# Hybrid decoder layer, one core: longer modelled waits and held order of the small products in the mixing stage

## The chip, the cores and the metric

One core of one Trainium2 chip runs the whole layer. The metric is device time in microseconds of one execution, the median of several runs; lower is better. Beside it stands one profiled execution, whose span and instructions the rows below show.

## The reference

The layer computes, in float32, for 512 tokens of 1024 columns: a SwiGLU half step, a mixing sub-layer of two branches, a second half step and a final norm. The mixing sub-layer is what the change touches.

```python
x = x + 0.5 * swiglu(rms_norm(x, ffn1_norm), ffn1_w_gate, ffn1_w_up, ffn1_w_down)
h = rms_norm(x, mix_norm)
p_rwkv, p_att, p_gate = split(h @ w_in)
y_rwkv = rwkv7_branch(p_rwkv, ...)     # 8 heads of 64; S_t = S diag(w) + (S a) b^T + v k^T, y = S r
y_att = attention_branch(p_att, ...)   # 8 query heads, 2 key heads, window 128, sinks
merged = sigmoid(gate_rwkv) * (y_rwkv @ w_branch_rwkv) + sigmoid(gate_att) * (y_att @ w_branch_attn)
x = x + merged @ w_out
x = x + 0.5 * swiglu(rms_norm(x, ffn2_norm), ffn2_w_gate, ffn2_w_up, ffn2_w_down)
return rms_norm(x, final_norm)
```

## The kernel before

**Layout.** Activations lie transposed: 128 columns of the layer on the partitions, 512 tokens along the free axis. A float32 product with weights ("dense") is done as three products of rounded parts: each weight tile is split into `wh` (a cast on ScalarE, ACT, L183) and `wl` (a subtraction on VectorE, DVE, L184), and `mm3` (L198 to L205) adds three TensorE (PE) products into one PSUM bank, `mm`. Raw weights come by DMA from the SP queue into three buffers `wr`.

**Stages.** The first half step fills the time to about 366 us, the mixing stage to about 725, the rest of mixing (branch and output projections) to about 816, then the second half step.

**Mixing stage.** The rwkv recurrence runs in blocks of 64 tokens (`C`), with two heads on the two halves of the partitions (h = 0 on 0 to 63, h = 1 on 64 to 127); four pairs of heads in all. Its small products use half or a quarter of the array each. Five generators ("lanes") hold the work:

- `lane_a`: attention's keys (`att_kv`), then four query pairs (`att`, L1178 on): the scores (L1191, L1193) into two banks `pS`, one per half; masking, exponentials, the scaling L1217, transposes (L1225), the output product (L1236, L1240) from `Pc` and `Pp`.
- `lane_p(0)`, `lane_p(1)`: for two pairs of heads each, `prep` (L809) and `solve` (L925). In `prep` the matrix G (L871 to L881) is made in two batches of eight products (four per half, L877), each half into a bank of its own; DVE masks both banks into `GT` (L880). `BK`, the stationary operand, is written for h = 0 and then h = 1 (L857, L862). Transposes of BK (L886) and the centred values `pvv` (L894) follow. `solve` inverts triangular blocks on DVE, with transfers through memory.
- `lane_w(0)`, `lane_w(1)`: `wkv` (L987): products p1 and p2 (L1003, L1012), three groups (L1029 to L1061), `pz` (L1070), six hops one after another (L1081, each followed by an ACT copy, L1083), the output product `py` (L1088, L1092), then the head norm.
- `head_sums` (L784) is used by all: ACT casts `hi` (L787), DVE makes `lo` (L789), and after a modelled wait of `WSUM` = 1200 PE runs L792 and L793.

**PSUM.** The small products share the tag `sm`: three banks for "a" (prep and lane_w(0)), three for "b" (attention and lane_w(1)). Dense products have one bank each of `mma` and `mmb`.

**Dense stream.** `dense_stream` (L707) walks through 42 jobs: k, r, v per pair of heads, K, V, q, sixteen gate tiles g, and eight b (which need attention's output). A job's two or four quarter steps are six products each, and count 1390 on the model's clock. At most two jobs ahead have their weights loaded.

**What sets the order.** `Counted` (L70) issues the small products and adds modelled nanoseconds to a clock. `interleave` (L87 to L108) is the planner: each lane yields a modelled wait and is ready again when the clock has passed it; a ready lane (in the order a, w0, w1, p0, p1) goes on; when none is ready, one dense step is emitted; a step more is emitted for each 3840 of credit. That is the traced order. The Tile scheduler then orders each engine's instructions: an instruction traced earlier goes first unless, in the scheduler's own forecast, its inputs or its buffer aren't ready yet; then a later one takes its place. The engines run that fixed order on the chip and wait wherever an input is late. `tc.keep_in_program_order(i)` binds an instruction behind the one traced just before it on the same engine; others may still come between the two.

The lines of the planner that the change touches:

```python
        wait = next(lanes[i], None)
        ...
        credit += RATIO * (pe.clock - before)
        ready[i] = pe.clock + wait
```

Of the kernel before, what the change touches and what calls it, by code (L numbers as in the profile page):

```python
# [15 lines left out]
P = 128  # L16
# [15 lines left out]
HD = 64  # L32
C = 64
# [22 lines left out]
HOP = 900.0  # L56

# [12 lines left out]
class Counted:  # L70


    def __init__(self, pe):
        self.pe, self.clock = pe, 0.0

    def matmul(self, out, lhsT, rhs, **k):
        self.pe.matmul(out, lhsT=lhsT, rhs=rhs, **k)  # L77

        half = lhsT.shape[0] <= HD or _free(lhsT) <= HD
        self.clock += 4 * max(_free(lhsT) / 2, _free(rhs)) / 2.4 * (0.55 if half else 1.0)  # L80

    def transpose(self, out, in_, ident):
        self.pe.transpose(out, in_, ident)  # L83
        self.clock += 2 * _free(in_) / 2.4


def interleave(lanes, pe, dense):  # L87
# [5 lines left out]
    while live:  # L93
# [11 lines left out]
        ready[i] = pe.clock + wait  # L105
# [13 lines left out]
def hybrid_layer_kernel(  # L119
# [625 lines left out]
    sp = Counted(pe)  # L745
# [63 lines left out]
    def prep(i):  # L809
# [177 lines left out]
    def wkv(i, sx):  # L987
# [12 lines left out]
        for n in range(NCH):  # L1000
            for h in (0, 1):
                r0 = h * HD
                sp.matmul(p1[r0 + 32:r0 + HD, n * 32:(n + 1) * 32], lhsT=GT[r0:r0 + 32, n // 2, h, n % 2, 32:],  # L1003
                          rhs=YTv[r0:r0 + 32, n, :], start=True, stop=True)
# [4 lines left out]
        for n in range(NCH):  # L1009
            for h in (0, 1):  # L1010
                r0 = h * HD
                sp.matmul(p2[r0:r0 + 32, n * 32:(n + 1) * 32], lhsT=YTv[r0 + 32:r0 + HD, n, :],  # L1012
                          rhs=GI[r0 + 32:r0 + HD, n, 32:64], start=True, stop=True)
# [12 lines left out]
        for n in range(NCH):  # L1026
            if n > 0:
                for h in (0, 1):
                    sp.matmul(pa[HS[h], n, :], lhsT=AR[HS[h], n, 0, :], rhs=ident[HS[h], HS[h]], start=True, stop=True)  # L1029
            for h in (0, 1):  # L1030
                sp.matmul(pv_[HS[h], n, :], lhsT=GT[OS[h], n // 2, h, n % 2, :], rhs=UV[OS[h], n, h, :],
                          start=True, stop=True)
# [6 lines left out]
        for n in range(NCH):  # L1039
            for h in (0, 1):  # L1040
                sp.matmul(pv_[HS[h], n, :], lhsT=GI[HS[h], n, :], rhs=xv[HS[h], n, :], start=True, stop=True)
        for n in range(1, NCH):
            for h in (0, 1):
                sp.matmul(pa[HS[h], n, :], lhsT=GI[HS[h], n, :], rhs=at_[HS[h], n, :], start=True, stop=True)
# [10 lines left out]
        for n in range(1, NCH):  # L1055
            for h in (0, 1):
                sp.matmul(pr_[HS[h], n, :], lhsT=AR[HS[h], n, 0, :], rhs=GT[HS[h], n // 2, h, 2 + n % 2, :],
                          start=True, stop=True)
            for h in (0, 1):
                if n + 1 < NCH:  # L1060
                    sp.matmul(pm[HS[h], n, :], lhsT=AR[HS[h], n, 0, :], rhs=GT[HS[h], n // 2, n % 2, 4 + h, :],  # L1061
                              start=True, stop=True)
# [360 lines left out]
```

## Time and profile before

| what | value |
|---|---|
| median of 3 runs | 1161.02 us (1157.81 to 1163.99) |
| profiled execution | 1161.56 us |
| its span in the profile | 1159.8 us |
| PE busy | 1118.2 us |
| DVE busy | 870.4 us |
| ACT busy | 585.7 us |

"Busy" is the time in which at least one instruction of the engine ran. In the names of groups, `sm<-AR,BK` is an output tile, the moving operand and the stationary one; a float32 product appears as two records, a transpose as one. L77 is the line in `Counted.matmul` through which all small products pass, so they are told apart by their tiles; L83 is that of the transposes. "64*128" is the part of the array that a product uses (rows by columns).

### The profile page before, as it was taken

Reading aid. Unit: us, or ns where it says so; the run is one execution under the profiler, and the core shown is the slowest. Engines: PE = TensorE matmul, PEld = TensorE weight load, DVE = VectorE, ACT = ScalarE, POOL = GpSimd, SP = SyncE. Lnnn points to the kernel's source line nnn. Section 1 sums busy time; section 2 is a strip of 40 time slices with the busy share of each in tenths; the row PEclk is TensorE's granted clock in tenths of the full one; section 3 lists DMA queues with packets and bytes.
Section 4 is the critical chain, followed back from the end, with each engine's and each line's share of the span. In section 5 each row is a group of like instructions: output and inputs, shape, how many; then the busy total and the mean of one; then the engine's idle time right before and its main releaser. Section 6 shows DMA issues by size and latency. Waiting matters only on the chain.

```text
span 1159.8 us, 19736 instructions
## 1 busy us (share of the span) xinstructions
PE 1118.2 (96%) x7866; PEld 970.1 (84%) x7866; DVE 870.4 (75%) x1138; ACT 585.7 (50%) x945; POOL 245.1 (21%) x175
## 2 busy tenths in 40 slices
PE   7899999999999999999998999999999999999997
PEld 6698899979987787777776788777999899989985
DVE  6988579856986589988886533878997379945875
ACT  5754155523645755566744445656655145523554
POOL 6231034202301000000111122121432024302200
PEclk9999999999999999999989999999999999999999
DMA  9234233432135534434235425852334223432221
GB/s 272 58 108 128 73 92 109 138 98 73 49 100 166 184 111 97 102 83 122 70 89 148 121 84 156 261 162 83 92 110 143 76 82 101 134 103 73 74 91 73
DMA packets 223068, 130.12 MB, mean 112 GB/s; under 512 B 37727, under 2 KB 204448, under 8 KB 222976
## 3 DMA queue, kind: packets, MB, share of 16 engines
q1 hardware_dynamic: 221248, 126.79, 38.2%
q10 hardware_dynamic: 1184, 2.04, 0.5%
q8 instruction: 62, 1.02, 0.4%
q14 instruction: 30, 0.25, 0.1%
q0 software_dynamic: 544, 0.04, 0.0%
HBM read 112.96 MB, written 15.61 MB: 111 GB/s over the span
## 4 chain that ended last, share of the span: by engine, by line
PE 72%; DVE 17%; DMA 5%; ACT 3%; issue 2%; SPq 1%; POOL 0%; ACTq 0%; DVEq 0%; POOLq 0%
PE sm L418 30%; PE mm L203 9%; PE mm L205 9%; PE mm L204 9%; PE sm L77 4%; PE sm L203 3%; PE sm L205 3%; PE sm L204 3%; DVE wl L184 3%; DVE pr L921 2%; DVE xt L377 1%; ACT wh L183 1%; PE sm L83 1%; DMA wr<-in_ffn_w_up_dram 1%; DMA wr<-in_ffn_w_gate_dram 1%
## 5 line engine op out<-in xcount | busy, mean ns | idle before, releaser
L184 DVE TENSOR_TENSOR wl<-wr,wh 128x1024 fp32r<-128x1024 f32 (+2 forms) x149 | 213.7, 1434 | 93.0 <-ACT wh L183 92.4
L183 ACT CAST wh<-wr 128x1024 fp32r<-128x1024 f32 (+2 forms) x149 | 147.5, 990 | 216.7 <-PE mm L204 98.7
L406 POOL TENSOR_TENSOR wx<-wr,wx 128x1024 f32<-128x1024 f32 x40 | 117.6, 2940 | 371.5 <-DVE wl L184 242.2
L418 PE MATMUL sm<-th,wh 128*128 128x256 f32 x640 | 180.9, 283 | 0.6 <-ACT s L429 0.3
L418 PE MATMUL sm<-tl,wh 128*128 128x256 f32 x640 | 180.2, 282 | 0.0
L418 PE MATMUL sm<-th,wl 128*128 128x256 f32 x640 | 180.2, 282 | 0.0
L184 DVE TENSOR_TENSOR wl<-wx,wh 128x1024 fp32r<-128x1024 f32 x100 | 157.6, 1583 | 26.9 <-ACT wh L183 26.2
L183 ACT CAST wh<-wx 128x1024 fp32r<-128x1024 f32 x100 | 104.9, 1049 | 131.9 <-PE sm L418 80.4
L418 PE MATMUL sm<-xh,wl 128*128 128x256 f32 x480 | 136.0, 283 | 0.8 <-DVE wl L184 0.8
L418 PE MATMUL sm<-xh,wh 128*128 128x256 f32 x480 | 136.0, 283 | 0.0
L418 PE MATMUL sm<-xl,wh 128*128 128x256 f32 x480 | 135.7, 283 | 0.0
L203 PE MATMUL mm<-xh,wh 128*128 128x512 f32 x320 | 130.9, 409 | 3.2 <-ACT wh L183 1.7
L205 PE MATMUL mm<-xh,wl 128*128 128x512 f32 x320 | 126.3, 395 | 1.0 <-DVE wl L184 1.0
L204 PE MATMUL mm<-xl,wh 128*128 128x512 f32 x320 | 126.4, 395 | 0.0
L418 PEld LDWEIGHTS sm<-th,wh 128*128 128x128 f32 x640 | 120.7, 189 | 1.7 <-issue 0.7
L418 PEld LDWEIGHTS sm<-tl,wh 128*128 128x128 f32 x640 | 120.6, 188 | 0.0
L418 PEld LDWEIGHTS sm<-th,wl 128*128 128x128 f32 x640 | 120.5, 188 | 0.0
L418 PEld LDWEIGHTS sm<-xh,wl 128*128 128x128 f32 x480 | 91.8, 191 | 1.3 <-DVE wl L184 1.3
L418 PEld LDWEIGHTS sm<-xh,wh 128*128 128x128 f32 x480 | 91.7, 191 | 0.5 <-issue 0.2
L418 PEld LDWEIGHTS sm<-xl,wh 128*128 128x128 f32 x480 | 91.7, 191 | 0.5 <-issue 0.2
L203 PEld LDWEIGHTS mm<-xh,wh 128*128 128x128 f32 x320 | 60.3, 189 | 19.0 <-issue 2.0
L205 PEld LDWEIGHTS mm<-xh,wl 128*128 128x128 f32 x320 | 60.5, 189 | 15.5 <-DVE wl L184 1.4
(387 smaller groups left out, 2289.8 us busy)
## 6 DMA issues: line engine op xcount, KB each, us to landing
wr<-in_ffn_w_down_dram SPq DMA_DIRECT2D x38, 512.0 KB, 4.0
wr<-in_w_in_dram SPq DMA_DIRECT2D x34, 512.0 KB, 4.2
wr<-in_ffn_w_gate_dram SPq DMA_DIRECT2D x42, 256.0 KB, 3.0
wr<-in_ffn_w_up_dram SPq DMA_DIRECT2D x42, 256.0 KB, 3.4
wx<-in_ffn_w_gate_dram SPq DMA_DIRECT2D x40, 256.0 KB, 3.1
wx<-in_ffn_w_up_dram SPq DMA_DIRECT2D x40, 256.0 KB, 3.5
gd<-gt SPq DMA_DIRECT2D x16, 256.0 KB, 2.3
wr<-in_w_out_dram SPq DMA_DIRECT2D x8, 512.0 KB, 5.5
```

What stands on the lines that cost most here:

```text
L77: self.pe.matmul(out, lhsT=lhsT, rhs=rhs, **k)
L83: self.pe.transpose(out, in_, ident)
L183: s.copy(out=hi[:, c], in_=raw[:, c])
L184: v.tensor_tensor(out=lo[:, c], in0=raw[:, c], in1=hi[:, c].bitcast(F32), op=ALU.subtract)
L203: pe.matmul(acc, lhsT=ah, rhs=bh, start=(first and k == 0), stop=False)
L204: pe.matmul(acc, lhsT=ah, rhs=bl, start=False, stop=False)
L205: pe.matmul(acc, lhsT=al, rhs=bh, start=False, stop=(last and k == n - 1))
L377: v.scalar_tensor_tensor(out=t_[:, 1 + i, :], in0=b0, scalar=g1, in1=b1, op0=ALU.mult, op1=ALU.add if i == 2 else ALU.subtract)
L406: e.tensor_tensor(out=o, in0=a, in1=b, op=op)
L418: pe.matmul(acc, lhsT=x_, rhs=y_, start=first and j == 0 and k == 0 and i == 0, stop=last and k == n - 1 and i == 2, skip_group_check=True)
L921: v.tensor_tensor(out=pv_[:, m], in0=a_[:, m].unsqueeze(2).broadcast_to(sh), in1=b_[:, m].rearrange("p u c -> p c u").unsqueeze(1).broadca ...
```

## The change

A constant `SLACK = 1.15, 200.0` is added, and the planner takes a modelled wait above 300 as 1.15 times the wait plus 200. `Counted` gets the tile context and a context manager `together`: within it, each small product but the first is bound behind the one traced before it. Eleven groups of small products are put into such a block: G's two batches, `pvv`, p1, p2, the four groups of `wkv` up to `pz`, `py`, the scores and the output product of attention. In G and in the first part of attention's output product the halves are traced h = 1 first, then h = 0. No operation is added or removed. The remaining hunks only indent other groups in the same way.

```diff
--- before.py
+++ after.py
@@ -54,6 +54,7 @@
 AHEAD = 2
 WSUM = 1200.0
 HOP = 900.0
+SLACK = 1.15, 200.0
 
 
 class InOrder:
@@ -70,17 +71,30 @@
 class Counted:
 
 
-    def __init__(self, pe):
-        self.pe, self.clock = pe, 0.0
+    def __init__(self, pe, tc):
+        self.pe, self.tc, self.clock, self.lump = pe, tc, 0.0, None
+
+    @contextmanager
+    def together(self):
+
+        self.lump = 0
+        yield
+        self.lump = None
+
+    def keep(self, i):
+        if self.lump is not None:
+            if self.lump:
+                self.tc.keep_in_program_order(i)
+            self.lump += 1
 
     def matmul(self, out, lhsT, rhs, **k):
-        self.pe.matmul(out, lhsT=lhsT, rhs=rhs, **k)
+        self.keep(self.pe.matmul(out, lhsT=lhsT, rhs=rhs, **k))
 
         half = lhsT.shape[0] <= HD or _free(lhsT) <= HD
         self.clock += 4 * max(_free(lhsT) / 2, _free(rhs)) / 2.4 * (0.55 if half else 1.0)
 
     def transpose(self, out, in_, ident):
-        self.pe.transpose(out, in_, ident)
+        self.keep(self.pe.transpose(out, in_, ident))
         self.clock += 2 * _free(in_) / 2.4
 
 
@@ -102,7 +116,7 @@
             live.remove(i)
             continue
         credit += RATIO * (pe.clock - before)
-        ready[i] = pe.clock + wait
+        ready[i] = pe.clock + (SLACK[0] * wait + SLACK[1] if wait > 300.0 else wait)
         while credit >= LUMP:
             d = next(dense, 0.0)
             credit = credit - d if d else 0.0
@@ -742,7 +756,7 @@
             yas.append((h_, l_))
 
     jobs = list(JOBS)
-    sp = Counted(pe)
+    sp = Counted(pe, tc)
     dense = dense_stream()
 
     def need(*whats):
@@ -871,11 +885,12 @@
         GT = slot("GT", (P, NCH // 2, 2, 6, C))
         for n2 in range(0, NCH // 2, 2):
             pg = [pssm().rearrange("p (n a c) -> p n a c", n=2, c=C) for h in (0, 1)]
-            for n in (n2, n2 + 1):
-                for m in (0, 1):
-                    for h in (0, 1):
-                        sp.matmul(pg[h][:, n - n2, m:4:2, :], lhsT=BK[HS[h], 2 * n + m, :, :],
-                                  rhs=AR[HS[h], 2 * n + m, :, :], start=True, stop=True)
+            with sp.together():
+                for n in (n2, n2 + 1):
+                    for m in (0, 1):
+                        for h in (1, 0):
+                            sp.matmul(pg[h][:, n - n2, m:4:2, :], lhsT=BK[HS[h], 2 * n + m, :, :],
+                                      rhs=AR[HS[h], 2 * n + m, :, :], start=True, stop=True)
             for h in (0, 1):
                 v.tensor_tensor(out=GT[:, n2:n2 + 2, h, 0:4, :], in0=pg[h],
                                 in1=gmask.unsqueeze(1).broadcast_to([P, 2, 4, C]), op=ALU.mult)
@@ -889,10 +904,11 @@
         yield 0.0
 
         pvv = pssm()
-        for n in range(NCH):
-            ns = slice(n * C, (n + 1) * C)
-            sp.matmul(pvv[HD:P, ns], lhsT=vm[0:HD, ns], rhs=cen[0:HD, :], start=True, stop=True)
-            sp.matmul(pvv[0:HD, ns], lhsT=vm[HD:P, ns], rhs=cen[HD:P, :], start=True, stop=True)
+        with sp.together():
+            for n in range(NCH):
+                ns = slice(n * C, (n + 1) * C)
+                sp.matmul(pvv[HD:P, ns], lhsT=vm[0:HD, ns], rhs=cen[0:HD, :], start=True, stop=True)
+                sp.matmul(pvv[0:HD, ns], lhsT=vm[HD:P, ns], rhs=cen[HD:P, :], start=True, stop=True)
         UV = slot("UV", (P, NCH, 2, C))
         s.copy(out=UV[HD:P, :, 0, :], in_=c3(pvv)[HD:P])
         v.tensor_copy(out=UV[0:HD, :, 1, :], in_=c3(pvv)[0:HD])
...
@@ -1183,14 +1206,15 @@
         S = slot("S2", (P, 2, NB, P))
         for b2 in (0, 1):
             pS = [pssm("b").rearrange("p (b a c) -> p b a c", b=2, a=2) for h in (0, 1)]
-            for bb in (0, 1):
-                b = 2 * b2 + bb
-                for h in (0, 1):
-                    qs, k_ = qn[HS[h], b * P:(b + 1) * P], kd[(kv + h) % 2][HS[h]]
-                    if b == 0:
-                        sp.matmul(pS[h][:, 0, 1, :], lhsT=qs, rhs=k_[:, 0:P], start=True, stop=True)
-                    else:
-                        sp.matmul(pS[h][:, bb, :, :], lhsT=qs, rhs=k_[:, (b - 1) * P:(b + 1) * P], start=True, stop=True)
+            with sp.together():
+                for bb in (0, 1):
+                    b = 2 * b2 + bb
+                    for h in (0, 1):
+                        qs, k_ = qn[HS[h], b * P:(b + 1) * P], kd[(kv + h) % 2][HS[h]]
+                        if b == 0:
+                            sp.matmul(pS[h][:, 0, 1, :], lhsT=qs, rhs=k_[:, 0:P], start=True, stop=True)
+                        else:
+                            sp.matmul(pS[h][:, bb, :, :], lhsT=qs, rhs=k_[:, (b - 1) * P:(b + 1) * P], start=True, stop=True)
             for h in (0, 1):
                 s.copy(out=S[:, h, 2 * b2:2 * b2 + 2, :], in_=pS[h][:, :, 1, :])
                 for bb in (0, 1):
@@ -1228,17 +1252,18 @@
             s.copy(out=Pp[:, h, 0:3 * P], in_=pT[:, P:4 * P])
         yield 2500.0
         po = pssm("b")
-        for b in range(NB):
-            bs = slice(b * P, (b + 1) * P)
-
-
-            for h in (0, 1):
-                sp.matmul(po[HS[h], bs], lhsT=vdv[:, b, kv * HD:(kv + 1) * HD], rhs=Pc[:, h, bs],
-                          start=True, stop=(b == 0))
-            for h in (0, 1):
-                if b > 0:
-                    sp.matmul(po[HS[h], bs], lhsT=vtv[:, b - 1, kv * HD:(kv + 1) * HD], rhs=Pp[:, h, (b - 1) * P:b * P],
-                              start=False, stop=True)
+        with sp.together():
+            for b in range(NB):
+                bs = slice(b * P, (b + 1) * P)
+
+
+                for h in (1, 0):
+                    sp.matmul(po[HS[h], bs], lhsT=vdv[:, b, kv * HD:(kv + 1) * HD], rhs=Pc[:, h, bs],
+                              start=True, stop=(b == 0))
+                for h in (0, 1):
+                    if b > 0:
+                        sp.matmul(po[HS[h], bs], lhsT=vtv[:, b - 1, kv * HD:(kv + 1) * HD], rhs=Pp[:, h, (b - 1) * P:b * P],
+                                  start=False, stop=True)
         o = slot("w", name="ya")
         s.copy(out=o, in_=po)
         dma.dma_start(out=yd_[(4 + i) * P:(5 + i) * P, :], in_=o)
```

## Rows read from the trace of the kernel before

**Rows 1.** The page, part 1: busy time (share of the span), instructions.

```profile
PE 1118.2 (96%) x7866; PEld 970.1 (84%) x7866; DVE 870.4 (75%) x1138; ACT 585.7 (50%) x945; POOL 245.1 (21%) x175
```

**Rows 2.** Stretches of the mixing stage: busy time by engine, clock, DMA.

```profile
core 0: us, PE busy (x) PEld busy (x) DVE busy (x) ACT busy (x) POOL busy (x), PEclk, DMA share, GB/s
428.00:620.00 192.00, 182.01 (x1732) 144.17 (x1732) 171.08 (x355) 107.73 (x246) 11.35 (x19) 0.97 0.39 93
620.00:690.00 70.00, 66.67 (x769) 53.84 (x769) 32.32 (x41) 31.98 (x58) 15.28 (x12) 1.00 0.42 117
690.00:724.80 34.80, 34.80 (x153) 28.28 (x152) 15.06 (x20) 18.23 (x33) 9.42 (x7) 1.00 0.47 146
```

**Rows 3.** Waits of PE, 428 to 690 us: total, times, longest.

```profile
PE sm L77 <- DVE GT L880: 3.9, 4, 1.2
PE sm L83 <- DVE S L1217: 2.8, 1, 2.8
PE sm L77 <- DVE AR L1076: 2.0, 1, 2.0
PE sm L793 <- DVE lo L789: 1.9, 2, 1.3
PE sm L792 <- ACT hi L787: 1.3, 1, 1.3
PE sm L77 <- DVE BK L862: 0.9, 2, 0.6
```

**Rows 4.** Timeline of PE, the second preparation's G: start, length, idle before in brackets.

```profile
455.46 2.34 PE L77 MATMUL sm<-AR,BK 64*128 64x128 f32 x24 [0.29 <-DVE BK L862]
458.74 1.16 PE L77 MATMUL sm<-AR,BK 64*128 64x128 f32 x8 [0.94 <-DVE GT L880]
```

**Rows 5.** Timeline of DVE, the same stretch.

```profile
457.34 0.74 DVE L1134 SCALAR_TENSOR_TENSOR w<-w,qkg,tb 128x512 f32<-128x512 f32 x1
458.00 2.62 DVE L880 TENSOR_TENSOR GT<-sm,gmask 128x512 f32<-128x512 f32 x4
```

**Rows 6.** Timeline of PE, attention scores: first lane, then the third.

```profile
463.13 0.92 PE L77 MATMUL sm<-w,qn 64*128 64x128 f32 x4
...
472.90 1.13 PE L77 MATMUL sm<-ks,qn 64*128 64x256 f32 x4
...
554.83 0.48 PE L77 MATMUL sm<-ks,qn 64*128 64x256 f32 x1
...
555.59 0.38 PE L77 MATMUL sm<-w,qn 64*128 64x256 f32 x1
```

**Rows 7.** Stretches at half clock, and one ahead of the first; columns as rows 2.

```profile
465.50:468.90 3.40, 3.40 (x8) 2.25 (x8) 3.40 (x9) 1.28 (x4) 0.04 (x1) 0.50 0.43 40
588.40:595.20 6.80, 6.80 (x51) 5.60 (x51) 4.58 (x13) 2.13 (x4) 0.00 (x0) 0.50 0.58 157
455.40:465.50 10.10, 9.10 (x91) 7.45 (x92) 10.02 (x18) 5.05 (x11) 0.42 (x2) 1.00 0.30 71
```

**Rows 8.** Timeline of PE around two small products issued alone.

```profile
576.27 0.43 PE L77 MATMUL sm<-Pc,vdif 128*64 128x128 f32 x2
...
614.23 0.24 PE L77 MATMUL sm<-YT,GT 32*32 32x32 f32 x2
614.40 0.50 PE L203 MATMUL mm<-xh,wh 128*128 128x512 f32 x1
614.74 0.39 PE L204 MATMUL mm<-xl,wh 128*128 128x512 f32 x1
614.97 0.39 PE L205 MATMUL mm<-xh,wl 128*128 128x512 f32 x1
```

**Rows 9.** Timelines of PE and ACT around the stage's end.

```profile
685.40 0.50 PE L203 MATMUL mm<-xh,wh 128*128 128x512 f32 x1
...
701.90 0.60 ACT L208 CAST xh<-o 128x512 fp32r<-128x512 f32 x1
...
724.76 0.39 PE L203 MATMUL mm<-xh,wh 128*128 128x512 f32 x1
```

More of the change, by code (lines that the diff above doesn't have):

```diff
@@ L1025, in wkv @@
         pa, pv_ = bank(), bank()
-        for n in range(NCH):
-            if n > 0:
+        with sp.together():
+            for n in range(NCH):
+                if n > 0:
+                    for h in (0, 1):
+                        sp.matmul(pa[HS[h], n, :], lhsT=AR[HS[h], n, 0, :], rhs=ident[HS[h], HS[h]], start=True, stop=True)
                 for h in (0, 1):
-                    sp.matmul(pa[HS[h], n, :], lhsT=AR[HS[h], n, 0, :], rhs=ident[HS[h], HS[h]], start=True, stop=True)
-            for h in (0, 1):
-                sp.matmul(pv_[HS[h], n, :], lhsT=GT[OS[h], n // 2, h, n % 2, :], rhs=UV[OS[h], n, h, :],
-                          start=True, stop=True)
+                    sp.matmul(pv_[HS[h], n, :], lhsT=GT[OS[h], n // 2, h, n % 2, :], rhs=UV[OS[h], n, h, :],
+                              start=True, stop=True)
         at_, xv = (slot("t").rearrange("p (n c) -> p n c", c=C) for _ in (0, 1))
@@ L1038, in wkv @@
         pa, pv_ = bank(), bank()
[L1039 to L1044, printed above, removed]
+        with sp.together():
+            for n in range(NCH):
+                for h in (0, 1):
+                    sp.matmul(pv_[HS[h], n, :], lhsT=GI[HS[h], n, :], rhs=xv[HS[h], n, :], start=True, stop=True)
+            for n in range(1, NCH):
+                for h in (0, 1):
+                    sp.matmul(pa[HS[h], n, :], lhsT=GI[HS[h], n, :], rhs=at_[HS[h], n, :], start=True, stop=True)
         v.tensor_copy(out=UV[HS[0], :, 0, :], in_=pv_[HS[0]])
@@ L1054, in wkv @@
         pr_, pm = bank(), bank()
[L1055 to L1061, printed above, removed]
+        with sp.together():
+            for n in range(1, NCH):
+                for h in (0, 1):
+                    sp.matmul(pr_[HS[h], n, :], lhsT=AR[HS[h], n, 0, :], rhs=GT[HS[h], n // 2, h, 2 + n % 2, :],
                               start=True, stop=True)
+                for h in (0, 1):
+                    if n + 1 < NCH:
+                        sp.matmul(pm[HS[h], n, :], lhsT=AR[HS[h], n, 0, :], rhs=GT[HS[h], n // 2, n % 2, 4 + h, :],
+                                  start=True, stop=True)
         v.tensor_tensor(out=at(0, 1), in0=pr_[:, 1, :], in1=AR[:, 1, 1, :], op=ALU.add)
@@ L1067, in wkv @@
         pz = pssm(sx).rearrange("p (n c) -> p n c", c=C)
-        for n in range(NCH - 1):
-            for h in (0, 1):
-                sp.matmul(pz[HS[h], n, :], lhsT=GT[:, n // 2, n % 2, 4 + h, :], rhs=UV[:, n, h, :], start=(n == 0),
-                          stop=(n == 0), skip_group_check=True)
+        with sp.together():
+            for n in range(NCH - 1):
+                for h in (0, 1):
+                    sp.matmul(pz[HS[h], n, :], lhsT=GT[:, n // 2, n % 2, 4 + h, :], rhs=UV[:, n, h, :], start=(n == 0),
+                              stop=(n == 0), skip_group_check=True)
         for h in (0, 1):
```

40 lines of the change are left out of this document (21 added, 19 removed).

## The prediction

> **What bounds the kernel now.** I read the page's engine lines first, then a table of stretches, then the waits of TensorE (PE), then the timelines around each wait. PE is busy 96% of the span [rows 1]: over the whole kernel the products set the time, so the change can only pay with PE time, idle or badly used, inside the mixing stage. The table of stretches splits that stage at three points [rows 2]. From 428 to 620 us PE is busy 182.0 of 192 us, but VectorE (DVE) 171.1 (89%): here both are near full, and the small products wait for DVE. From 620 to 690 PE is busy 66.7 of 70 and DVE only 32.3. From 690 to 724.8 PE has no idle at all: dense products alone, after the last small product of the last pair of heads. So the stage is packed unevenly: lanes and DVE early, a dense tail late.
>
> The waits of PE between 428 and 690 us are few [rows 3]: 3.9 us in four waits for the masked copy of G (L880), 2.8 for the softmax scaling L1217, 2.0 for L1076, 1.9 + 1.3 for the two halves of a head sum (L789, L787), 0.9 for L862; with a last one of 0.4 that makes 13.2 us. The span is 1159.8 us and that execution took 1161.56 us, 0.5 above the median of the runs shown (1161.02); I sum against 1161.5 and take the 0.5 off at the end.
>
> **Part 1: G in alternating halves (L877), four times 16 products.** In the second preparation PE ran 12 products (24 records) in 2.34 us, waited 0.94 us for L880, and ran the last 4 in 1.16 us [rows 4]; the other three look the same, the fourth at half clock. The last four are all of one half: its bank had to be emptied first. So four products of one half cost 1.16 us. What a pair costs is seen at the scores of attention, same operand form (64 rows by 128 columns): two products of one half 1.13 us, but four products (eight records, the first and the last shown) with the halves alternating from 554.83 to 555.97, 1.14 us [rows 6]. A pair takes the time of one. Sixteen products as eight pairs then take 2 x 1.16 = 2.32 us in place of 2.34 + 1.16 = 3.50: 1.18 us each, 4.7 us for four. Starting with h = 1, whose bank and whose half of BK come last, moves the wait ahead of the whole batch, where the scheduler may put dense products; that could free the 3.9 us too. Best end: 8.6 us.
>
> The other end is DVE. Between the first and second batch DVE had three other operations in front of L880 (the last of them at 457.34), and L880 began at 458.00 [rows 5], 2.5 us after the batch began. A faster first batch does not move those. Unless dense work fills the hole, the second batch starts where it does now and only its own 1.16 - 0.95 = 0.2 us is won, 0.8 in all (0.95 is the batch without its tail, an estimate from the 1.16). Between 0.8 and 8.6 I take 5: DVE is as full here as rows 2 say, but the wait now stands where dense products can be put in.
>
> The Trainium skill, page "TensorEngine Tiling (Array Packing)", section Performance Considerations, says that packing speeds TensorE up and not the emptying of PSUM, so the copy can become the bottleneck. By that rule Part 1 gives its low end; the rows on L880 agree with it so far, and it is my first rival below.
>
> **Part 2: the scores of attention (L1191, L1193).** Only the first of the four attention lanes ran them half by half: about 0.92 twice and 1.13 twice at full clock, 4.1 us [rows 6]; paired, 0.92 + 1.14 = 2.06. Gain 2.0 us, from 1.0 (bank of the second half still late) to 3.0 (the fourth lane, partly split, joins).
>
> **Part 3: pieces of a group.** A group whose first product is ready early is issued alone, and dense work then comes between. One product of p1 (2 records) at 614.23 delays the dense one by 0.17 us and the dense pair after it starts 0.34 us apart instead of the 0.23 usual among dense ones [rows 8]: some 0.25 us a piece. The reversed order (h = 1 first) cures it at the output product (L1236), which was torn in three of four lanes (one of them at 576.27, in the same rows); p1 and p2 keep theirs. Gain 0.5, between 0 and 2. The held order of the remaining groups (L894, L1029 to L1092) is nearly what ran before; I cost it at nothing, covered by the dense products beside it. Nothing on SP, ACT or POOL's queues is moved by these edits themselves.
>
> **Part 4: longer modelled waits.** A modelled wait w above 300 becomes 1.15 w + 200. The planner fills waits with dense steps of 1390, so only rounding matters: 1200 (the head sums) becomes 1580 and asks for two steps instead of one; 5000 (before L1217) becomes 5950, five instead of four; 1500 (before the first hop) becomes 1925, still two; 1000 becomes 1350, still one; the hops, 900, become 1235, still one. Of rows 3 that reaches the head sums (3.2 us, take 2.5) and L1217 (2.8, take 2.0), and not L1076 or L862: 4.5 us, between 0 and the 9.3 that are not G's.
>
> I also worked the planner's loop through with the prices in the code, in dense steps done out of 152. The last product of the four pairs of heads stands at step 57, 76, 107, 124 before and 62, 80, 114, 135 after; the lanes end at 129 and at 142. As a check: 28 steps after the last product, 38.9 us of model, and the trace has 39.4 us from 685.40 (the first dense product behind L1092) to 724.76, the first product of the next stage [rows 9]. So the lanes stretch by a tenth and the dense tail shrinks by 11 steps, 15.3 us, to 24.1. Dense work is used up nowhere. The cover that this takes away: after the last small product the chain of normalisation, scaling and splitting runs to the cast of the last `xh`, which ends at 702.50, and its low half, estimated 0.7 more: 17.8 us [rows 9]. 24.1 still hides it, with 6.3 to spare. Cost 0, up to 5 if the lanes slip further. More dense steps between small ones mean more changes of form: 13 more at most, each about 0.2 us by rows 8: cost 1.5, from 0 to 2.6.
>
> **Part 5: clock.** Twice the granted clock stood at half in this stretch, 465.5 to 468.9 and 588.4 to 595.2 [rows 7], 1.2 instead of 2.4 GHz; 10.2 us at half rate cost 5.1. Ahead of the first, PE was busy 9.10 of 10.1 us while DVE was busy 10.02: small products at DVE's pace. With dense work in those holes one of the two may go: gain 2.5, from 5.1 to a loss of 3.4 (two more such falls).
>
> **Part 6: new waits.** Every DVE, ACT and queue order in the stage is drawn anew. No row shows the waits of that layout; the nearest is the present sum, 13.2 us. Bounds 0 and 9; I take 3, nearer the low end because the lanes are less crowded.
>
> **Sum:** -5.0 - 2.0 - 0.5 - 4.5 + 1.5 - 2.5 + 3.0 = -10.0. 1161.5 - 10.0 - 0.5 = 1151.0 us.
>
> **Rivals.**
> 1. DVE paces G and the head sums, and PE's saving becomes waiting: Part 1 gives 0.8, Part 4 about 2, the clock nothing, new waits 3, changes of form 1.5: net -2.0 - 0.5 - 0.8 - 2 + 4.5, about -1 to -3: 1158.5. For it: rows 5 and the 89%. Against it: between 620 and 690 DVE has room, and the planner moves work there. The same time results if the scheduler tears the groups as before. Chance 0.24.
> 2. Slower: the tail. If the lanes slip on the chip as much again as in the planner (15.3 us more), the cover is 8.8 us against a chain of 17.8, and PE stands 9 us before the next stage. That happens if DVE can't keep the dense splits, now placed ahead of the lanes, and the lanes as well; then Parts 1 and 4 give nothing either: +9 - 2.5 + 1.5 + 3 = +11, 1172. It costs from a slip of 21.6 us on (39.4 - 17.8); it outweighs my gain when the slip passes 32. Against it: DVE is under half busy after 620. Chance 0.10.
> 3. It bites harder: all of G's 8.6, half the other waits, both half-clock stretches, no new waits: -8.6 - 2.5 - 1 - 6 - 5.1 + 1 = -22: 1139. Chance 0.12.
>
> **How the numbers follow.** Forecast (a gain of 6 to 16 us, 1145 to 1155): 0.54, and the likeliest. A measurement of this kernel can tell about 0.5%, 5.8 us, from no change. Faster by more than that: 0.54 + 0.12 = 0.66; within: 0.24; slower: 0.10. The range takes in the forecast's band, rival 1 with Part 6 at its bound, and rival 3's upper part: 1139 to 1163; rival 2 and the far half of rival 3 stay outside.
>
> **What would show it.** G: 16 products in two runs of about 1.1 us, dense products between them, and less than 2 us of waits for L880; if those waits are 5 us or more, rival 1. The head-sum and L1217 waits gone, L1076's still there. The clock at full around the first two G's. Dense tail after the last L1092 about 24 us, DVE's share between 428 and 620 near 80%, between 620 and 690 above half. Wrong would be a PE gap ahead of the first product of the next stage (rival 2), or a sum of waits above 13 us in the stage.

## The result, and the profile after

| what | before | after |
|---|---|---|
| median of 9 runs each, side by side | 1157.81 us (1154.31 to 1163.99) | 1150.23 us (1149.44 to 1153.23) |
| ratio of the medians, 95% interval | | 0.9926 [0.9912, 0.994] |
| profiled execution | 1161.56 us | 1149.44 us |
| its span | 1159.8 us | 1147.4 us |

The change makes the kernel 0.74% faster, and the whole interval lies beyond the 0.5% that can be told from no change. The forecast, 10.0 us off 1161.0, is a ratio of 0.9914, inside the interval. The two profiled executions differ by 12.1 us, more than the medians do (7.6): that of before was 3.8 us above its median, that of after 0.8 below. So the sums below, made on these two traces, are too large by some 4 us; the two profiles of before in the table below show which terms are the loose ones.

The page of after, part 1, for [rows 1]:

```profile
PE 1107.3 (97%) x7866; PEld 961.3 (84%) x7866; DVE 868.8 (76%) x1138; ACT 586.2 (51%) x945; POOL 246.3 (21%) x175
```

The same instructions, and PE busy 10.9 us less: most of the gain is time in which PE runs, not waits that are gone. The stretches, for [rows 2], with the same columns (the tail's stretch ends earlier, at 712):

```profile
428.00:620.00 192.00, 181.36 (x1739) 142.18 (x1742) 170.53 (x354) 110.00 (x247) 14.18 (x21) 0.98 0.40 99
620.00:690.00 70.00, 68.74 (x815) 56.38 (x814) 31.16 (x42) 29.30 (x56) 15.31 (x12) 1.00 0.41 115
690.00:712.00 22.00, 22.00 (x95) 17.54 (x94) 14.10 (x19) 16.91 (x30) 6.93 (x5) 1.00 0.59 179
```

From 428 to 620 nothing looks different: DVE is as full as it was, PE as well. In the second stretch PE stands 1.3 us where it stood 3.3, and issues 815 records in place of 769. The waits of PE between 425 and 690 us, for [rows 3]:

```profile
PE sm L91 <- DVE GT L895: 3.4, 3, 1.3
PE sm L91 <- ACT AR L1067: 1.5, 2, 1.2
PE sm L91 <- DVE YT L1013: 1.4, 1, 1.4
PE sm L91 <- DVE BK L876: 1.4, 2, 1.0
PE sm L97 <- DVE S L1241: 1.3, 1, 1.3
PE sm L91 <- DVE S L1222: 0.7, 1, 0.7
PE sm L807 <- DVE lo L803: 0.7, 1, 0.7
PE mm L219 <- DVE wl L198: 0.6, 1, 0.6
PE sm L97 <- DVE GT L895: 0.6, 1, 0.6
```

Line numbers have moved: L77 is L91 now, L83 L97, the masked copy L880 is L895, L862 is L876, L1217 is L1241, L789 is L803, L1076 is L1098. The masked copy still holds PE for 4.0 us. The head sums lost most of their waits (0.7 of 3.2 is left), L1241 half, and L1098 is not in the list at all. In their place stand L1067, L1013, L1222, L198 and 0.5 us more of `BK`. The wait for L1076 (2.0 us in [rows 3]) is also missing from the second profile of before, whose other waits are nearly the same, so its going can't be put down to the change.

G of the second preparation, for [rows 4] (the timeline of PE, start and length in us, with the dense products between the two parts) and for [rows 5] (that of DVE):

```profile
451.57 1.38 PE L91 MATMUL sm<-AR,BK 64*128 64x128 f32 x18 [0.39 <-DVE BK L876]
452.88 0.50 PE L218 MATMUL mm<-xl,wh 128*128 128x512 f32 x1
...
456.83 1.16 PE L91 MATMUL sm<-AR,BK 64*128 64x128 f32 x14 [1.14 <-DVE GT L895]
...
528.71 1.16 PE L91 MATMUL sm<-AR,BK 64*128 64x128 f32 x16
...
551.21 1.16 PE L91 MATMUL sm<-AR,BK 64*128 64x128 f32 x16
```

```profile
451.75 0.67 DVE L305 TENSOR_TENSOR w<-tb,w 128x512 f32<-128x512 f32 x1
452.35 1.01 DVE L937 TENSOR_TENSOR pr<-Y,U 64x512 f32<-64x512 f32 x1
453.29 0.68 DVE L308 SCALAR_TENSOR_TENSOR tb<-w,tb 128x512 f32<-128x512 f32 x1
453.89 0.67 DVE L939 TENSOR_REDUCE V<-pr 64x64 f32<-64x512 f32 x1
454.48 0.73 DVE L1157 SCALAR_TENSOR_TENSOR w<-w,qkg,tb 128x512 f32<-128x512 f32 x1
455.14 1.03 DVE L937 TENSOR_TENSOR pr<-V,Y 64x512 f32<-64x512 f32 x1
456.09 0.68 DVE L895 TENSOR_TENSOR GT<-sm,gmask 128x512 f32<-128x512 f32 x1
```

Sixteen products now take 1.38 + 1.16 = 2.54 us where they took 3.50, and eleven dense ones were put between the two parts. The wait ahead of the second part is there all the same, 1.14 us for 0.94: the masked copy began 4.5 us after the batch and not 2.5 as before, behind six other operations of DVE. The first and the fourth preparation have the same two parts; the third ran its two batches whole, 1.16 us each and far apart (the last two lines), with no wait.

An output product of attention, and the end of the stage (timelines of PE and ACT), for [rows 8, 9]:

```profile
573.01 0.66 PE L91 MATMUL sm<-Pc,vdif 128*64 128x128 f32 x8
...
573.72 0.39 PE L91 MATMUL sm<-Pc,vdif 128*64 128x128 f32 x4
...
574.15 0.39 PE L91 MATMUL sm<-Pc,vdif 128*64 128x128 f32 x4
...
687.32 1.03 PE L91 MATMUL sm<-GT 64*64 64x64 f32 x28
...
712.78 0.40 PE L217 MATMUL mm<-xh,wh 128*128 128x512 f32 x1
```

```profile
703.46 0.62 ACT L222 CAST xh<-o 128x512 fp32r<-128x512 f32 x1
```

The group that was torn from 576.27 on runs in one piece, 1.5 us from end to end (between its lines stand its other products, those of `Pp`). The last products of `py` end at 688.35; the next stage begins at 712.78, 12.0 us earlier than at 724.76, with no PE wait ahead of it; the cast of the last `xh` is over at 704.08.

**Where the time went.** From the first product of G to the first product of the next stage I put each stretch between the starts of two products (both records of one counted together) into three sorts: the time in which PE ran, the time in which it stood after the last end, and what half clock added (half of the running time in stretches where the granted clock was 1.2 GHz). One execution each, in us:

| kernel | stage | PE ran | PE stood | half clock |
|---|---|---|---|---|
| before | 297.0 | 278.5 | 13.3 | 5.1 |
| before, a second profile (below) | 297.9 | 277.7 | 12.0 | 8.2 |
| after | 284.1 | 268.8 | 11.8 | 3.4 |

Of the 9.7 us of running, G gave 3.5 (12.90 to 9.36), the attention scores 1.2 (10.20 to 9.00), the output product of attention 1.2 (7.89 to 6.72), and the other groups of small products 3.4 together. The dense ones count 0.4 less only because 10 of 750 now run ahead of the first G, 2.4 us; each costs a little more, 0.2453 for 0.2425, which is 2.0 us over 740. The two profiles of before show how firm each column is: 0.8 us in what PE ran, 1.3 in the waits, 3.1 in the clock. The gain in running is beyond that; those in the last two columns are not shown to be.

### The profile page after: what moved, and what is told of

It reads as the page before. It is cut to its first block, busy times and chain, and to the rows that moved or that the text cites. A ratio compares the mean times of both kernels' runs of the same rounds, so it can differ in the third digit from the quotient of the medians.

```text
span 1147.4 us, 19742 instructions
## 1 busy us (share of the span) xinstructions
PE 1107.3 (97%) x7866; PEld 961.3 (84%) x7866; DVE 868.8 (76%) x1138; ACT 586.2 (51%) x945; POOL 246.3 (21%) x175
## 4 chain that ended last, share of the span: by engine, by line
PE 72%; DVE 17%; DMA 4%; ACT 3%; issue 3%; SPq 0%; POOL 0%; ACTq 0%; DVEq 0%; POOLq 0%
PE sm L432 30%; PE mm L217 9%; PE mm L218 9%; PE mm L219 9%; PE sm L91 4%; DVE wl L198 3%; PE sm L219 3%; PE sm L217 3%; PE sm L218 3%; DVE pr L937 1%; ACT wh L197 1%; DVE xt L391 1%; DMA wr<-in_ffn_w_up_dram 1%; DMA wr<-in_ffn_w_gate_dram 1%; DVE t L475 1%
## 5 line engine op out<-in xcount | busy, mean ns | idle before, releaser
L198 DVE TENSOR_TENSOR wl<-wr,wh 128x1024 fp32r<-128x1024 f32 (+2 forms) x149 | 214.2, 1438 | 88.0 <-ACT wh L197 87.1
L198 DVE TENSOR_TENSOR wl<-wx,wh 128x1024 fp32r<-128x1024 f32 x100 | 157.6, 1583 | 26.9 <-ACT wh L197 26.2
```

Source lines behind the costliest of these rows:

```text
L198: v.tensor_tensor(out=lo[:, c], in0=raw[:, c], in1=hi[:, c].bitcast(F32), op=ALU.subtract)
```

## Experiments

All kernels here compute everything. They ran in three groups, and each ratio is to the runs of before in the same group. The median of before was 1159.44 us for the first group (waits alone, order alone, G alone, order with halves not turned), 1158.98 for the second (the whole change not turned, more credit, still longer waits, mask off DVE) and 1159.28 for the third (the rest).

The theory that I began with, A: the held order gives most of the gain, since G and the scores are the largest terms. Its rival, B: the longer modelled waits give most.

**The longer waits alone**, on the kernel before:

```diff
+SLACK = 1.15, 200.0
...
-        ready[i] = pe.clock + wait
+        ready[i] = pe.clock + (SLACK[0] * wait + SLACK[1] if wait > 300.0 else wait)
```

> The kernel before with the longer modelled waits alone; the small products stay free in their order. Theory A (the held order gives most of the gain: in the pair of profiles the small products took 9.3 us less of PE between the first G and the next stage, its waits only 1.5 us less and the half clock 1.7 less): 1153 to 1158 against about 1158 of before, G still torn into single halves, its 16 products 3.2 us a time. Theory B (the later lanes give most, since a less crowded stage lets the scheduler keep the halves together by itself): 1149 to 1152, dense tail after the last small product about 24 us. The dense tail should be about 24 us by both, as it is set by the planner.

Measured: 1153.2 us, 0.994 [0.9917, 0.9963]. PE ran 271.4, stood 10.7, half clock 3.4.

The waits of PE in this kernel (its lines are those of before plus one):

```profile
PE sm L78 <- DVE GT L881: 3.4, 3, 1.6
PE sm L84 <- DVE S L1218: 1.6, 1, 1.6
...
PE sm L793 <- ACT hi L788: 0.7, 1, 0.7
```

So without any order held, the head sums and L1218 already wait nearly as little as in after, and 7.1 of the 9.7 us of running are there: G gives only 0.6, the scores 1.7, the rest 4.7 (the output product 0.75, the head sums 0.65). Fewer groups are torn: along the timeline of PE the output product of attention comes in 5 pieces for its four lanes (8 in before, 4 in after), the scores, eight batches, in 9 (12 in before, 11 in after). G is still run in single halves in three of four preparations. That a lane now finds all its inputs there when it goes on is how I read it; no run shows that step by itself.

**The held order alone** (the change with the waits as before):

```diff
-SLACK = 1.15, 200.0
+SLACK = 1.0, 0.0
```

> The changed kernel with the modelled waits as before: held order and turned halves alone. Theory A: 1150 to 1153 (the 9.3 us of small products without the 1.5 of waits and with the clock as it falls), G's 16 products about 2.3 us a time, waits of PE in the stage 12 to 15 us, tail about 39 us. Theory B: 1155 to 1159; the order alone only turns PE time into waits for VectorE, over 17 us of waits in the stage.

Measured: 1157.85 us, 0.9982 [0.9965, 0.9999]. PE ran 273.6, stood 15.1, half clock 5.1. Its waits on the masked copy and on the head sums:

```profile
PE sm L91 <- DVE GT L895: 4.4, 4, 1.7
PE sm L807 <- DVE lo L803: 2.5, 2, 2.1
PE sm L97 <- DVE GT L895: 1.9, 2, 1.7
```

G's products gain the same 3.5 us as in after, but the copy is waited for 6.3 us where before waited 3.9. It is this run that goes against A, by nearly 5 us. The first alone did not decide: 1153.2 is at the lower edge of what A expected and above B's, and G was still torn, as A had it. Put together, the longer waits gave 0.6% and the held order 0.2%, which also add up to the change, so B holds as to which is the larger share.

**G alone held and turned**, with waits as before and no other group held:

```diff
-            for n in (n2, n2 + 1):
-                for m in (0, 1):
-                    for h in (0, 1):
+            with sp.together():
+                for n in (n2, n2 + 1):
+                    for m in (0, 1):
+                        for h in (1, 0):
```

> The kernel before with held order and turned halves in the two batches of G alone. Theory A: G's share of the products is 3.5 of 9.3 us: 1154 to 1155.5, with G's waits for the masked copy still 4 to 5 us. Rival (VectorE paces G, so a faster G only waits longer): 1157 to 1159, G's waits 7 us or more.

Measured: 1156.76 us, 0.9979 [0.9965, 0.9993]; PE ran 274.0, stood 13.7, half clock 1.7. The time lies between what the two sides expected. The waits are nearer the rival's: 6.0 us for the masked copy (4.0 ahead of G, 2.0 ahead of the transposes) and 1.7 for `BK`. All that the held order is worth is in G, as far as these intervals can tell.

**Held order, halves not turned** (the previous but one, with h = 0 first):

```diff
-                        for h in (1, 0):
+                        for h in (0, 1):
...
-                for h in (1, 0):
+                for h in (0, 1):
```

> As the order alone, but with h = 0 traced first everywhere. Theory A1 (the binding makes the halves alternate, whichever comes first): within 1.5 us of the order alone, G alternating, only some first products issued alone with dense ones behind them. Rival (the first product, issued early because its half is ready first, pulls the whole bound group to the front, where PE waits for the late half): 3 us or more above the order alone, with the waits of G's first batch for BK up from 1.4 to 3 us or more.

Measured: 1155.9 us, 0.9966 [0.9953, 0.9979]; PE ran 276.4, stood 14.7, no half clock at all in the stage. **The same on the whole change** (longer waits, order held, halves not turned):

> The changed kernel with h = 0 traced first everywhere, held order and longer waits kept. The order alone gave 0.9982 of before with the halves turned and 0.9966 without. Theory F (turning the halves does nothing that can be told, the held order makes them alternate either way): 1149 to 1152, within 1.5 us of the changed kernel. Rival (turning them keeps first products from being issued alone): 1152.5 or more.

Measured: 1152.81 us, 0.994 [0.9919, 0.9961]; PE ran 269.1, stood 13.0, half clock 3.4. G's products take 10.35 and 10.17 us in these two, 9.35 and 9.36 with the halves turned: about a microsecond in the trace. In the times the two pairs point opposite ways (2.0 us faster without the turning, 2.6 slower; both had been expected within 1.5), and their intervals overlap. The granted clock can account for most of both: averaged over all runs of each kernel it was 0.9955 without and 0.9941 with the turning in the first pair, 0.9925 and 0.9943 in the second, at most 1.6 and 2.1 us of the 1150 (an estimate: the share of the clock that was missing, times the span). So no worth of the turning is shown in the times.

Next: why do longer waits help? B1: because more dense steps lie between the steps of the lanes, however they come there. Its rival: because the right waits, those of the head sums and L1217, got longer.

**More dense credit** (on the kernel before, nothing else changed):

```diff
-RATIO = 0.65
+RATIO = 0.8
```

> The kernel before with the planner's credit ratio at 0.8 instead of 0.65, waits and order as before. Worked through by the planner's loop, the last products of the four pairs of heads then stand at dense steps 60, 80, 112, 135 of 152 and the lanes end at 140, nearly as with the longer waits (62, 80, 114, 135; 142), but by dense work added to the products and not to the waits. Theory B1 (what pays is that the lanes are spread over more dense work): 1152 to 1155, as the longer waits alone (ratio 0.994). Rival B2 (what pays is the longer pause between a producer and its product): 1157 to 1161, no change that can be told.

Measured: 1153.91 us, 0.9948 [0.993, 0.9965]; PE ran 276.5, stood 6.5, half clock 6.7. Stretches (columns as [rows 2]) and waits of PE:

```profile
428.00:620.00 192.00, 185.99 (x1687) 146.96 (x1685) 170.94 (x340) 111.44 (x249) 13.00 (x20) 0.96 0.42 103
620.00:690.00 70.00, 70.00 (x807) 57.20 (x804) 35.03 (x58) 27.93 (x53) 17.77 (x13) 1.00 0.38 106
```

```profile
PE sm L83 <- DVE S L1217: 3.1, 2, 2.1
PE sm L77 <- DVE GT L880: 0.9, 2, 0.7
```

No wait was lengthened, and yet the time fell nearly as far: the waits for G's copy went from 3.9 to 0.9, and PE had no idle from 620 to 690. So B1 holds as far as the time goes. The gain is another one, though: credit took off 6.8 us of standing and 2.0 of running, where the longer waits took off 2.6 and 7.1. G's products even cost 1.2 us more than in before. L1217's own wait stayed at 3.1, so a longer wait at that place does something that credit doesn't. Which of the longer waits counts was not tried one by one.

**Still longer waits**, the mechanism of rival 2:

```diff
-SLACK = 1.15, 200.0
+SLACK = 1.3, 400.0
```

> The changed kernel with waits of 1.3 w + 400. By the planner's loop the dense steps are used up (152 of 152) before the lanes end and 13.7 us of model pass with nothing to do. Theory (the second rival of the prediction: past the point where the dense tail no longer covers the lanes' end, PE stands): 1163 to 1178, with PE gaps of 10 us or more ahead of the first product of the next stage, and fewer waits than 11.7 us before them. Rival (the scheduler's own order keeps dense work back, and the waits go down further): 1146 to 1152.

Measured: 1172.19 us, 1.0107 [1.0081, 1.0133]. PE around the stage's end, and ACT:

```profile
716.70 0.81 PE L91 MATMUL sm<-GT 64*64 64x64 f32 x18
721.67 0.80 PE L806 MATMUL sm<-hi,bones 128*128 128x512 f32 x1 [4.17 <-ACT hi L801]
...
732.52 0.80 PE L217 MATMUL mm<-xh,wh 128*128 128x512 f32 x1 [9.32 <-ACT xh L222]
```

```profile
731.85 0.62 ACT L222 CAST xh<-t 128x512 fp32r<-128x512 f32 x1 [3.38 <-DMA t<-yd__3948]
```

The last product of `py` starts at 717.3, 29 us later than in after, and by then no dense product is left: nothing covers the chain from there to the cast that ends at 732.47. PE stands 4.2 and 9.3 us, 13.5 of the 16.0 by which it stands longer in this stage than in after. G's products take 9.2 us in this kernel and the scores 7.9, no longer than in after: most of the waiting that is new lies in the tail. Half clock adds some 3.5 us more than in after, the last of it in a stretch that begins at 719.1, while PE stands.

**Is it DVE that holds G?** Theory D: the masked copy waits in DVE's queue, and without it there G's waits go. The copy out of PSUM moved to ACT, the mask to GpSimd (on the kernel after):

```diff
-                v.tensor_tensor(out=GT[:, n2:n2 + 2, h, 0:4, :], in0=pg[h],
-                                in1=gmask.unsqueeze(1).broadcast_to([P, 2, 4, C]), op=ALU.mult)
+                gh = GT[:, n2:n2 + 2, h, 0:4, :]
+                s.copy(out=gh, in_=pg[h])
+                g.tensor_tensor(out=gh, in0=gh, in1=gmask.unsqueeze(1).broadcast_to([P, 2, 4, C]), op=ALU.mult)
```

> The changed kernel with G copied out of PSUM by ScalarE and masked in place by GpSimd, in place of one VectorE product; the rest as in the changed kernel. Theory D (G's second batch waits for VectorE's queue, in which four to seven other operations stand ahead of the copy): the waits of PE for G's copy fall from 4.0 us to under 1.5, time 1146 to 1149. Rival (the wait is set by something else, or ScalarE's queue is as full): waits of 3 us or more for the copy, 1149 to 1153.

Measured: 1166.24 us, 1.0056 [1.0037, 1.0074], far above what both sides expected. The waits of PE (lines are those of after, plus one from the copy on):

```profile
PE sm L806 <- ACT hi L801: 4.7, 1, 4.7
PE sm L97 <- ACT GT L896: 3.2, 2, 2.7
```

The longer of the two waits that make up the 3.2 us, in the first preparation (timelines of PE and ACT):

```profile
436.19 0.63 ACT L843 ACTIVATE g<-g 128x512 f32<-128x512 f32 x1 [2.19 <-DVE g L840]
...
437.87 0.66 PE L97 MATMUL sm<-ident,BK 128*128 128x128 f32 x4 [2.69 <-ACT GT L896]
```

The wait ahead of G's own products did go, from 4.8 us with `BK` to 1.5, but the transposes behind them, which need the same banks, waited 3.2 for ACT's copy. PE stood 21.6 us in all, some 14 of them for ACT and some 7 for DVE, and half clock added 7.6 us, 4.2 more than in after. ACT takes 0.59 us for such a copy and GpSimd 1.49 for the mask; the masked copy took 0.68 on DVE, so DVE was not slow at it. In these places it was the operations ahead of the copy that delayed it: six on DVE, and on ACT, in the lines above, one that itself waited 2.2 us for DVE.

**DVE loaded more** (after, with a plain copy of the same size ahead of each masked one):

```diff
+                v.tensor_copy(out=GT[:, n2:n2 + 2, h, 0:4, :], in_=pg[h])
                 v.tensor_tensor(out=GT[:, n2:n2 + 2, h, 0:4, :], in0=pg[h],
```

> The changed kernel with one more VectorE copy of the same bank in front of each masked copy of G (16 more operations of about 0.68 us, 10.9 us of VectorE). Theory D (VectorE's queue paces the second batch of G and, being near full until 620 us, the lanes): PE's waits for G's copies rise from 4.0 us to 7 to 10, time 3 to 7 us above the changed kernel, 1153 to 1157. Rival (VectorE has room, the waits are only a matter of order): 1149.5 to 1152.5.

Measured: 1153.01 us, 0.9948 [0.9929, 0.9967], just inside what Theory D expected of the time. Waits of PE:

```profile
PE sm L91 <- DVE GT L896: 3.7, 2, 2.8
PE mm L217 <- DVE pt L620: 3.4, 1, 3.4
PE mm L219 <- DVE wl L198: 1.8, 1, 1.8
PE sm L91 <- DVE BK L876: 1.7, 2, 1.0
```

Sixteen copies of 0.68 us are 10.9 us more on DVE. G's waits rose from 5.4 to 5.8 us (both with `BK` and the transposes), while two dense products waited 5.2 us for DVE. Theory D had the copy's waits rise to 7 us or more; with the transposes they are 4.1, so its mechanism is not what the trace shows. In all PE stood 12.8 us, 1.0 more than in after. The interval overlaps that of after, and the mean granted clock of its runs is lower, 0.9915 for 0.9943, which can make up to 3.2 us, more than the 2.8 between the medians. So no price of the added load is shown.

**Both ways of spreading at once**, on the kernel after:

```diff
-RATIO = 0.65
+RATIO = 0.75
```

> The changed kernel with the credit ratio at 0.75: by the planner's loop the lanes end at step 145 instead of 142 and the last products stand at 64, 90, 113, 138 (62, 80, 114, 135), which leaves 14 dense steps, 19.5 us, after the last small product. Theory C (spreading pays until the tail is as long as the chain of 15 to 18 us that it covers): 1148 to 1151, no wait ahead of the next stage. Rival (the optimum is past already): 1152 to 1157, with a gap before the next stage's first product.

Measured: 1151.08 us, 0.9934 [0.9915, 0.9953]: the same as after, and within 0.1 us of Theory C's range, with no wait ahead of the next stage. The last product of `py` starts at 695.0 and the next stage at 715.3; 20.3 us still cover the chain.

**Credit and held order**, on the kernel after:

```diff
-RATIO = 0.65
+RATIO = 0.8
...
-SLACK = 1.15, 200.0
+SLACK = 1.0, 0.0
```

> The changed kernel's held order and turned halves with the waits as before and the credit ratio 0.8. Theory (spreading the lanes and holding the order are two gains that add: 0.9948 for the ratio alone, 0.9982 for the order alone): ratio 0.992 to 0.994, 1149.5 to 1152. Rival (they overlap: both mend the same torn pieces): 1153 to 1155, as the ratio alone.

Measured: 1153.76 us, 0.9948 [0.9926, 0.997]: what the credit gave by itself, as the rival expected. PE ran 270.4, stood 14.2, half clock 1.7. Its waits:

```profile
PE sm L97 <- DVE S L1241: 3.0, 2, 2.1
PE sm L91 <- DVE GT L895: 2.8, 2, 1.7
```

Put beside the credit alone, the held order saved 6.1 us of running and cost 7.7 of waiting. It did the same, in smaller size, in the two other pairs: 4.9 saved and 1.8 lost on the kernel before, 2.6 saved and 1.1 lost on the kernel with the longer waits. Each of these is one execution, but the direction is the same three times, and the medians agree that the order by itself is worth little (0.2% or less).

**Before once more**, one profile, for the spread of the table above:

> The kernel before once more, for a second profile of the same program. If the 12.9 us between the two profiles from the first G to the next stage is the change's alone, the stage is again 296 to 298 us here; if part of it was luck of that execution (waits of 13.3 us and 10.2 us at half clock), the stage is 292 to 295 us, with the same order and the same pieces on PE.

Measured: 1159.4 us; its row is the second of that table. The stage took 297.9 us, with the same order and the same pieces, so the shorter stage is not luck of the first execution.

## Why the prediction was right, and which of its steps were not

The time, the sign and the main way (dense steps spread between the lanes, groups that run whole, a tail that still covers its chain) came as forecast. The terms did not all, and that their sum came out so near is in part luck: products, waits and clock missed to both sides.

- **Part 1, G**: taken at -5.0, between -0.8 and -8.6. The products: 4.7 forecast (2.32 for 3.50 us, four times), 3.5 measured; in three preparations the two parts take 2.54, and only in the third 2.32. The other 0.3 of the term was to come from the wait, which the batch's new beginning would move to where dense work could fill it. That step failed: three banks let the first product of the second batch out with the first batch in three preparations (18 records and 14, not 16 and 16; the banks are my reading of it), the rest waited, and G's waits, transposes included, went from 4.8 to 5.4 us. The sign named for it, less than 2 us for the masked copy, failed: 4.0. Dense work did fill the hole, but DVE took its other six operations first. Rival 1 was half right: DVE keeps its pace. Its price was wrong, since the dense products in the hole are a gain even so. By the Trainium skill, page "TensorEngine Tiling (Array Packing)", section Performance Considerations, packing does not speed up the emptying of PSUM; the 4.0 us of waits for the copy, 3.9 before, agree. The same section advises to use ScalarE beside VectorE for it; no run here shares the copies between the two. With all of them on ACT the kernel was 0.56% slower than before.
- **Part 2, the scores**: -2.0 taken, -1.2 measured, inside the bounds of 1.0 and 3.0 [rows 6]. Three batches of two lanes, from 459.32, 467.03 and 541.21 us, still came in two pieces each. The longer waits alone, with no order held, gave 1.7 here: the held order, in which I had put the gain, was not needed for it.
- **Part 3, torn groups**: taken at -0.5, at most -2, and the largest miss: all small products other than G and the scores run 4.6 us shorter. I looked for the cure in the order (h = 1 first) and counted the output product; the longer waits alone gave 4.7. I had seen the pieces as fixed, where they depend on how early a lane goes on. Part 4 had the means to see it: its own rounding turns the modelled 2500 ahead of the output product into 3075, three dense steps for two, and its list leaves that wait out. With the longer waits alone three of that product's four lanes came whole, where one had in before; that wait was not lengthened by itself.
- **Part 4, waits**: the head sums gave 2.5 (2.5 taken), L1217 1.5 (2.0 taken). L1076, which the rounding argument left alone, went from 2.0 to nothing, but the second profile of before doesn't have that wait either. Behind L862 the modelled 1200 becomes 1580 as well, which Part 4 doesn't count, and that wait grew all the same, from 0.9 to 1.4. More changes between dense and small products: 16 (139 to 155 along the timeline) for 13 at most, and 2.0 us for the 1.5 taken, if all that the dense products lost is put down to them.
- **Part 5, clock**: -2.5 taken, -1.7 measured. The granted clock fell to 1.2 GHz from 459.2 to 466.0 us, straight after the second G, in about the place of [rows 7], so the sign of a full clock around the first two G's failed. Ahead of it PE was busy 85% of the stretch and DVE throughout:

```profile
449.00:459.20 10.20, 8.67 (x65) 6.91 (x63) 10.14 (x20) 4.16 (x8) 0.00 (x0) 1.00 0.14 32
459.20:466.00 6.80, 6.80 (x50) 5.18 (x49) 5.07 (x12) 3.85 (x9) 0.53 (x3) 0.50 0.24 49
```

  Between two profiles of before this term differs by 3.1 us, so the profiles show neither the size nor the sign of 1.7. The granted clocks of all executions say a little more: on average 0.9943 over the nine of after, 0.9927 over the 56 of before that ran beside the experiments (none is on record for the nine beside after). That is up to 1.9 us over the whole kernel (an estimate: 0.0016 of 1155 us, as if PE ran all the time). So some gain by the clock is likely; that it came from dense work in DVE's holes is not shown.
- **Part 6, new waits**: +3.0 taken; with `BK` and the transposes about 5.3 (1.1 of it is in G's 5.4 above). One of them, 1.4 us for L1013, holds up p1: its first product starts at 615.36 and the others wait until 617.04, with no dense product between, where some stood in [rows 8]. All waits together: -1.8 in my sum (0.3 of G's, 4.5, and 3.0 back), -1.5 measured, hardly more than the 1.3 between two profiles of before. Right in total, by parts that missed to both sides.
- **The tail**: 24.1 us forecast, 24.6 from the start of the last product of `py`, and no wait. The lanes were to end a tenth later, counted in dense steps; in time the last `py` ended 2.9 us later, at 688.35 for 685.5, while the dense work behind it shrank by 15 us: the dense steps now between the lanes were nearly paid for by small products that run shorter.
- **DVE's share**: forecast near 80% up to 620 and above half after; it is 89% and 45%, as before. The lanes' own work on DVE hardly moved from the one stretch to the other.
- **Rival 2** didn't come, and its mechanism is real: with still longer waits the cover is gone and PE stands 9.3 us ahead of the next stage (9 forecast). That this kernel took 1172.19 us, and the rival's forecast was 1172, is luck: the rival had Parts 1 and 4 give nothing, and here G's products gave 3.7 us while PE stood 27.8 in the stage.
- **The rivals' sums** are loose: the terms of rival 1 add up to -0.8 and not -1 to -3, and rival 3 takes 6 for half of waits that are 9.3 in all.

Sum by the traces: running of small products -9.3, dense ones +2.0, waits -1.5, half clock -1.7 in the stage and -1.7 ahead of it (a fall at 369.9 us in the profile of before that after's doesn't have): -12.2, for 12.0 between the two starts of the next stage. Without the two clock terms it is -8.8, inside the 6.9 to 10.2 us that the interval of the ratio makes of 1157.81. So the forecast of -10.0 hit with terms for G, the scores and the clock that were too large or are not shown at their size, and a term for torn groups that was 4 us too small.

## What to carry to other kernels

Where a planner lays independent work between dependent steps, look first whether the groups of dependent products come out whole: a modelled wait that is too short shows not only as a wait but as torn groups, which count as busy time. Spreading the independent work wider pays until the last dependent chain is no longer covered. Here longer waits mended mainly the torn groups and more credit mainly the waits; put together in one kernel they gave no more than the longer waits with the held order had given, and the point where it turns is read from the tail. Holding a group in order saved running time here, and gave part or all of it back as waiting on the slowest input. Before a small difference is put down to such a change, the granted clock of the runs is worth a look: here it can account for 2 or 3 us between kernels that are otherwise close.

## What the runs showed of the hardware

The first dense product behind a change of the array's form (the part of it that a product uses) costs more than the next: after a 32-by-32 group of p1 (a sixteenth of the array, not the half or quarter that the description of the kernel gives for all small products) the dense products start 0.34 us apart and then 0.23 again (617.66, 618.00, 618.23 in the timeline of PE of after).

```profile
617.66 0.50 PE L217 MATMUL mm<-xh,wh 128*128 128x512 f32 x1
618.00 0.40 PE L218 MATMUL mm<-xl,wh 128*128 128x512 f32 x1
618.23 0.39 PE L219 MATMUL mm<-xh,wl 128*128 128x512 f32 x1
```

The Trainium skill, page "TensorEngine Tiling (Array Packing)", section Tiling Modes, says that a change of mode drains TensorE; the 0.11 us agree with it, though no row shows the drain by itself. What I had not expected is that a copy's own length hardly mattered here: 0.68 us on DVE, 0.59 on ACT, and the wait for it went by what stood in front of it, six operations on DVE and one that waited 2.2 us on ACT.
